# Expert products in four 32-column tiles, a two-part gather, and a ring of 14 weight slots

## The chip, the cores and the metric

The kernel runs on one core of a Trainium2 chip. The metric is the device time of one execution in microseconds. The kernel before took 1646.06 us, the median of three runs (1644.56 to 1650.3). The profiled execution took 1643.47 us, with a span of 1641.8 us from its first to its last instruction. In the rows, PE is the matmul engine, PEld its loading of the stationary operand, DVE, ACT and POOL the vector, scalar and general engines, SP the engine that issues the weight transfers.

## What is computed

Two transformer blocks over 256 tokens of width 1024. Each has a mixer (differential attention, a gated linear recurrence and an mLSTM, gated and merged); the first has a dense feed-forward layer, the second a mixture of eight experts, of which each token uses two. The change lies in the mixture:

```python
def _swiglu(h, w1, w3, w2):
    return (jax.nn.silu(h @ w1) * (h @ w3)) @ w2

def _moe(h, router_w, router_b, w1, w3, w2):
    logits = (h @ router_w).astype(f32) + router_b.astype(f32)
    probs = jax.nn.softmax(logits, axis=-1)
    top_p, top_i = lax.top_k(probs, TOP_K)                  # TOP_K = 2
    top_p = top_p / jnp.sum(top_p, axis=-1, keepdims=True)
    combine = jnp.sum(jax.nn.one_hot(top_i, N_EXPERTS) * top_p[..., None], axis=-2)
    out = jnp.zeros_like(h)
    for e in range(N_EXPERTS):                              # 8
        out = out + combine[..., e:e + 1] * _swiglu(h, w1[e], w3[e], w2[e])
    return out
```

Here `h` is 256 x 1024 (the norm of x, scaled and shifted), and the weights of an expert are 1024 x 2816 twice and 2816 x 1024, all float32.

## The kernel before

**Stages.** Mixer 0, the dense layer and mixer 1 take the first 877 us. Then come the routing (`moe_route`) and the eight experts (`moe_pass`), one after the other, and the output. Up to the end of mixer 1 all large products are made of float32r operands split into a high and a low part; the experts' products are float32 matmuls, which the trace shows as two records each.

**Weights.** An expert reads 35 loads ("raws"), each a transfer of 128 partitions x 2 rows of k x 1024 columns (1 MiB), or x 768 columns (768 KiB) for the last column group of W1 and W3. They come in this order: three column groups g = 0, 1, 2 of 1024, 1024 and 768 columns; in each, four loads of W1, then four of W3; then eleven loads of W2. `Stream.loads` (L78) issues a transfer on SP as soon as a slot of the ring is free. The ring has three pools: `rawa` (4 slots, from the start), `rawb` (5, opened four units before the end of mixer 1, L1696) and `rawc` (7, opened when the pools of the mixer close, L1703). A slot is free again when PE has used its load (`release`). The first nine loads are issued during the end of mixer 1, the next seven when the routing starts.

**Routing.** `moe_route` (L1287) takes the norm's scale `r` per token (a sum on DVE, a power on POOL), makes diagonal matrices `dg` of it on ACT, multiplies x with them into transposed blocks, scales and shifts these (`hf`, by turns on DVE and ACT), and multiplies with the router. The softmax, the two largest and the position of each token within its expert's list follow on DVE, with five small matmuls. Four iotas on POOL (`key`) stand ahead of the power.

**Gather.** `dispatch(e0)` (L1380) builds for two experts at a time a 0/1 matrix of tokens by places, multiplied with `r`; `gather(e0, j)` (L1394) multiplies x (128 tokens x 128 columns, stationary) with it, 256 columns wide, float32, and `xg`, the expert's tokens, scaled and shifted, is written from the sum. The gather for experts 0 and 1 stands ahead of the first expert; that for 2 and 3, 4 and 5, 6 and 7 lies in the W2 loads 4 to 7 of experts 1, 3 and 5.

**Products.** An expert has CAP = 128 places. The tokens are the stationary operand, the weights the moving one. With 64 tokens (HALF) stationary, the array takes two tiles of 64 columns side by side, each with half the load's columns; with 32 (QUART), four tiles of 32, each with a quarter. `passes` (L1458) makes for each load the products of the first 64 tokens always, in two tiles. What is left is decided on the chip by `more` (L1442) from the expert's count, with branches: over 96 tokens, the same again for places 64 to 127 (`half`); 65 to 96, the places 64 to 95 in four tiles (`quart`); at most 64, nothing (`rest`, only the second k-row of the first product). In column group 2 there is no `quart`: 65 to 96 tokens take `half` there, since 768 was not split into quarters (`quarters` is false for g = 2). This is the part of `passes` that makes the tiles:

```python
            def tiles(bank, kind, k, m):
                c = n // (128 // m)
                for q in range(128 // m):
                    PE.matmul(out=bank[m * q:m * q + m, 0:c], lhsT=lhs(kind, k), rhs=w[:, k, c * q:c * q + c],
                              start=first and k == 0, stop=last and k == 1)
```

After each column group the hidden values are transposed for W2 (`transposes`, L1488), three or four blocks of 128 columns for each of the two halves of the places. `scatter` (L1563) multiplies the expert's result back to the tokens' order and adds it to the sum `acc`; it runs in the second load of the next expert.

**Order.** The instructions of the experts are put in order by the scheduler of the tile framework from the code's order; near the end of expert 0 it places a few loads of expert 1 between those of expert 0.

Of the kernel before, what the change touches and what calls it, by code (L numbers as in the profile page):

```python
# [15 lines left out]
OP = mybir.AluOpType  # L16
# [161 lines left out]
MB = dict(small=4, rs=1, rt=1, ix=1, cm=1, fl=1, key=1, dg=1, pg=2, ps=2, xg=1, s=MS, gt=2, gt2=1, dT=2, mfs=2, acc=1)  # L178
RB = 5
RC = 7  # L180
# [10 lines left out]
def _body(ctx, tc, nc, I, out):  # L191
# [1095 lines left out]
    def moe_route():  # L1287
# [67 lines left out]
        cur["moe"] = dict(r=r, rt=rt, cm=cm, key=key, quart=quart)  # L1355

    def moe_pass(stream, off, raw_pool, finish):
# [22 lines left out]
        def dispatch(e0):  # L1380
            m = cur["moe"]
# [12 lines left out]
        def gather(e0, j):  # L1394
            pt = disp[e0]
# [46 lines left out]
        def more(e, half, quart, none=lambda: None):  # L1442
# [4 lines left out]
            with tc.If(num[e] > HALF) as c:  # L1447
                if quart is None:
                    half()
                else:  # L1450
                    with tc.If(num[e] > HALF + QUART) as c2:
                        half()
                    with c2.Else():
                        quart()
# [3 lines left out]
        def passes(e, banks, w, n, lhs, first, last, quarters):  # L1458

            def tiles(bank, kind, k, m):  # L1460
                c = n // (128 // m)
                for q in range(128 // m):
                    PE.matmul(out=bank[m * q:m * q + m, 0:c], lhsT=lhs(kind, k), rhs=w[:, k, c * q:c * q + c],  # L1463
                              start=first and k == 0, stop=last and k == 1)

            def rest():
                tiles(banks[0], 0, 1, HALF)

            def half():
                for k in range(2):  # L1470
                    tiles(banks[1], 1, k, HALF)
                rest()

            def quart():
                for k in range(2):
                    tiles(banks[1], 2, k, QUART)
# [264 lines left out]
```

## Time and profile before

| | |
|---|---|
| median of three runs | 1646.06 us (1644.56 to 1650.3) |
| profiled execution | 1643.47 us, span 1641.8 us |
| PE busy over the span | 1535.2 us (94%) |
| DVE, ACT, POOL busy | 764.9, 575.7 and 42.5 us |
| moved by the transfers | 459.25 MB, mean 280 GB/s |
| first product of expert 0, of expert 7 | 901.87 us, 1521.44 us from the span's start |
| last product of expert 7 | starts at 1626.14 us |

PE is busy nearly throughout, but that share hides that the transfers run at over 400 GB/s in a part of the expert stage and not in others. So the stage is read stretch by stretch: which of PE and DMA has no pause there. Matmul records overlap one another, so that a mean duration of one is more than its part of the time; the time of a run of records divided by their count gives the price.

### The profile page before, as it was taken

What the parts mean: (1) busy time and instruction counts of PE and PEld (TensorE: products, weight loads), DVE (VectorE), ACT (ScalarE), POOL (GpSimd) and SP (SyncE); (2) the same over time, 40 slices, a digit from 0 to 9 for tenths busy, and PEclk for the clock granted to TensorE, in tenths of its full rate; (3) what the DMA queues carried; (4) which work ended last, traced back from release to release, by engine and by line L of the source; (5) the groups of instructions that cost most, each with busy time, mean ns of one, the idle gap of its engine ahead of it and who ended that gap; (6) DMA issues with size and microseconds to landing.
All of it is one profiled execution on the core that took longest, in us unless ns stands there. A gap on an engine that the chain in (4) does not pass through costs nothing. (4 is left out here: it accounts for less than half of the span.)

```text
span 1641.8 us, 25655 instructions
## 1 busy us (share of the span) xinstructions
PE 1535.2 (94%) x10586; PEld 1069.2 (65%) x10586; DVE 764.9 (47%) x1226; ACT 575.7 (35%) x904; POOL 42.5 (3%) x54
## 2 busy tenths in 40 slices
PE   3999999989999899999997999999999988987997
PEld 2999899989998899999996333433334322322332
DVE  7898788755877559865764010211012111111201
ACT  3576557645444487765752010100001000100000
POOL 2001020000000000001000000000000000000000
PEclk9999999999999999999998999999999999999999
DMA  9656777436789633654467799999899999999990
GB/s 361 231 177 217 244 267 259 155 103 226 240 296 320 228 129 129 219 168 154 155 214 299 260 352 354 407 406 321 319 329 407 403 408 405 407 403 407 404 372 36
DMA packets 162776, 459.25 MB, mean 280 GB/s; under 512 B 11454, under 2 KB 19716, under 8 KB 162600
## 3 DMA queue, kind: packets, MB, share of 16 engines
q1 hardware_dynamic: 162408, 456.55, 75.7%
q8 instruction: 140, 2.29, 0.6%
q14 instruction: 36, 0.29, 0.1%
q0 software_dynamic: 192, 0.11, 0.0%
HBM read 455.58 MB, written 1.05 MB: 278 GB/s over the span
## 5 line engine op out<-in xcount | busy, mean ns | idle before, releaser
L1463 PE MATMUL pm<-rawa,xg 128*64 128x512 f32 (+2 forms) x2368 | 417.8, 522 | 21.1 <-DMA rawa<-in_moe_w 18.6
L113 DVE TENSOR_TENSOR wl<-rawa,wh 128x1024 fp32r<-128x1024 f32 (+1 forms) x243 | 293.9, 1215 | 103.1 <-ACT wh L112 102.2
L112 ACT ACTIVATE wh<-rawa 128x1024 fp32r<-128x1024 f32 (+1 forms) x243 | 255.2, 1054 | 229.9 <-PE pm L518 117.3
L1463 PEld LDWEIGHTS pm<-rawa,xg 128*64 128x64 f32 (+1 forms) x2368 | 141.6, 131 | 280.0 <-issue 225.9
L517 PE MATMUL pm<-hh,wh 128*128 128x256 f32 x992 | 285.4, 288 | 4.8 <-ACT hh L499 4.6
L518 PE MATMUL pm<-hl,wh 128*128 128x256 f32 x992 | 283.8, 287 | 0.9 <-DVE hl L500 0.9
L519 PE MATMUL pm<-hh,wl 128*128 128x256 f32 x992 | 283.0, 286 | 1.5 <-DVE wl L113 1.5
L517 PEld LDWEIGHTS pm<-hh,wh 128*128 128x128 f32 x992 | 189.0, 191 | 8.1 <-ACT hh L499 4.8
L519 PEld LDWEIGHTS pm<-hh,wl 128*128 128x128 f32 x992 | 189.1, 191 | 2.4 <-DVE wl L113 1.9
L518 PEld LDWEIGHTS pm<-hl,wh 128*128 128x128 f32 x992 | 189.3, 191 | 1.9 <-DVE hl L500 1.4
L1463 PE MATMUL px<-rawa,gt 128*64 128x512 f32 x704 | 168.0, 600 | 12.5 <-DMA rawa<-in_moe_w 12.3
L1534 DVE TENSOR_TENSOR esg<-esg,pm 128x512 f32<-128x512 f32 (+1 forms) x48 | 29.5, 641 | 297.7 <-PE pm L1463 297.4
L531 PE MATMUL pm<-wl,hh 128*128 128x256 f32 x448 | 128.7, 287 | 1.6 <-DVE wl L113 1.6
L530 PE MATMUL pm<-wh,hh 128*128 128x256 f32 x448 | 128.8, 288 | 0.0
L532 PE MATMUL pm<-wh,hl 128*128 128x256 f32 x448 | 127.8, 285 | 0.0
L1463 PEld LDWEIGHTS px<-rawa,gt 128*64 128x64 f32 x704 | 46.1, 136 | 107.8 <-issue 83.8
L393 DVE SCALAR_TENSOR_TENSOR macc<-rawm,csil,macc 128x1024 f32<-128x1024 f32 x74 | 94.6, 1279 | 30.8 <-DMA rawm<-in_w_mod 30.1
L531 PEld LDWEIGHTS pm<-wl,hh 128*128 128x128 f32 x448 | 85.1, 190 | 2.0 <-DVE wl L113 1.8
L1561 DVE COPY ys<-pm 128x512 f32<-128x512 f32 x8 | 5.5, 691 | 173.2 <-PE pm L1463 93.9
L532 PEld LDWEIGHTS pm<-wh,hl 128*128 128x128 f32 x448 | 85.0, 190 | 0.2 <-issue 0.2
L530 PEld LDWEIGHTS pm<-wh,hh 128*128 128x128 f32 x448 | 85.0, 190 | 0.0
L1497 ACT ACTIVATE gt<-px 128x512 f32<-128x512 f32 (+1 forms) x24 | 13.5, 564 | 197.3 <-PE px L1495 197.3
(370 smaller groups left out, 1940.6 us busy)
## 6 DMA issues: line engine op xcount, KB each, us to landing
rawa<-in_moe_w SPq DMA_DIRECT2D x216, 1024.0 KB, 17.1
rawa<-in_w_in SPq DMA_DIRECT2D x68, 1024.0 KB, 6.3
rawa<-in_moe_w SPq DMA_DIRECT2D x64, 768.0 KB, 12.0
rawm<-in_w_mod SPq DMA_DIRECT2D x80, 512.0 KB, 7.6
rawa<-in_ffn_w SPq DMA_DIRECT2D x29, 1024.0 KB, 7.6
rawa<-in_w_branch SPq DMA_DIRECT2D x12, 1024.0 KB, 5.7
rawa<-in_w_out SPq DMA_DIRECT2D x8, 1024.0 KB, 5.7
rawa<-in_w_mod SPq DMA_DIRECT2D x7, 1024.0 KB, 10.2
```

Source lines behind the costliest of these rows:

```text
L112: nc.scalar.activation(out=hv, in_=src, func=AF.Copy)
L113: nc.vector.tensor_sub(out=lv, in0=src, in1=hv.bitcast(F32))
L393: V.scalar_tensor_tensor(out=st["acc"], in0=src[:, 0], scalar=csil[:, k:k + 1], in1=st["acc"], op0=OP.mult, op1=OP.add)
L517: PE.matmul(out=o, lhsT=wh, rhs=xh[:, k], start=(k == 0), stop=False)
L518: PE.matmul(out=o, lhsT=wh, rhs=xl[:, k], start=False, stop=False)
L519: PE.matmul(out=o, lhsT=wl, rhs=xh[:, k], start=False, stop=(k == nk - 1))
L530: PE.matmul(out=o, lhsT=xh[:, k, c], rhs=wh, start=(k == 0), stop=False)
L531: PE.matmul(out=o, lhsT=xh[:, k, c], rhs=wl, start=False, stop=False)
L532: PE.matmul(out=o, lhsT=xl[:, k, c], rhs=wh, start=False, stop=(k == nk - 1))
L1463: PE.matmul(out=bank[m * q:m * q + m, 0:c], lhsT=lhs(kind, k), rhs=w[:, k, c * q:c * q + c], start=first and k == 0, stop=last and k == 1)
L1497: A.activation(out=gT[g][:, i], in_=pv, func=AF.Copy)
L1534: V.tensor_tensor(out=gt[g][:, b, c], in0=gt[g][:, b, c], in1=hp[1][b][:, c], op=OP.mult)
```

## The change

1. All products of the experts are made in four tiles of 32 columns. For the kinds of 64 tokens (first and second half of the places), tiles 0 and 1 take tokens 0 to 31 and 32 to 63 with the first half of the load's columns, tiles 2 and 3 the same with the second half. Each tile streams as many columns as before (512, or 384 in group 2); there are four matmuls where there were two.
2. `quart` exists in group 2 as well, with 192 columns a tile. The hidden values of that group then lie in another arrangement, so the transposes of the second half (`odd`) have a branch of their own for 65 to 96 tokens: two transposes and two half-high products, one with `ident` and one with `turn`, the identity rotated by 32 columns.
3. The gather takes x times r in a high and a low part, float32r (`xh`, `xl`), with a 0/1 matrix in float32r: per block two products in place of one float32 one. The parts are made once in `moe_route`, on ACT and DVE; the copy of `r` that was kept falls away.
4. The ring has 14 slots in place of 16 (`RC`, 7 to 5).

```diff
-RC = 7
+RC = 5
@@ moe_route
-        r0, dg = norm_scale(Sp)
-        r = M.tile([128, 2], F32, name="rs", tag="rs")
-        V.tensor_copy(out=r, in_=r0)
+        turn = M.tile([128, CAP], F32, name="turn", tag="turn")
+        G.tensor_copy(out=turn[:, 0:CAP - QUART], in_=ident[:, QUART:CAP])
+        G.tensor_copy(out=turn[:, CAP - QUART:CAP], in_=ident[:, 0:QUART])
+        r, dg = norm_scale(Sp)
...
+        xh = M.tile([128, 2, D], F32R, name="xrh", tag="xrh")
+        xl = M.tile([128, 2, D], F32R, name="xrl", tag="xrl")
+        for b in range(2):
+            A.activation(out=xh[:, b], in_=x[:, b], func=AF.Copy, scale=r[:, b:b + 1])
+            V.scalar_tensor_tensor(out=xl[:, b], in0=x[:, b], scalar=r[:, b:b + 1], in1=xh[:, b].bitcast(F32),
+                                   op0=OP.mult, op1=OP.subtract)
@@ dispatch
-                p_ = M().tile([128, 2, CAP], F32, name="pg", tag="pg")
-                idx = index(b, e0, 2)
-                for i in range(2):
-                    V.tensor_scalar(out=p_[:, i], in0=iota, scalar1=idx[:, i:i + 1], scalar2=m["r"][:, b:b + 1],
-                                    op0=OP.is_equal, op1=OP.mult)
+                p_ = M().tile([128, 2, CAP], F32R, name="pg", tag="pg")
+                V.tensor_tensor(out=p_, in0=index(b, e0, 2).unsqueeze(2).to_broadcast([128, 2, CAP]),
+                                in1=iota.unsqueeze(1).to_broadcast([128, 2, CAP]), op=OP.is_equal)
@@ gather
-                    PE.matmul(out=pv[:, k2], lhsT=x[:, b, c], rhs=pt[b].rearrange("p a s -> p (a s)"),
-                              start=(b == 0), stop=(b == 1))
+                    for i, src in enumerate((m["xh"], m["xl"])):
+                        PE.matmul(out=pv[:, k2], lhsT=src[:, b, c], rhs=pt[b].rearrange("p a s -> p (a s)"),
+                                  start=(b == 0 and i == 0), stop=(b == 1 and i == 1))
@@ passes
-            def tiles(bank, kind, k, m):
-                c = n // (128 // m)
-                for q in range(128 // m):
-                    PE.matmul(out=bank[m * q:m * q + m, 0:c], lhsT=lhs(kind, k), rhs=w[:, k, c * q:c * q + c],
-                              start=first and k == 0, stop=last and k == 1)
+            def tiles(bank, kind, k):
+                parts = 4 if kind == 2 else 2
+                c = n // parts
+                for q in range(4):
+                    t = q if kind < 2 else 0
+                    h = q * parts // 4
+                    o = QUART * (t % 2)
+                    PE.matmul(out=bank[QUART * q:QUART * q + QUART, 0:c], lhsT=lhs(kind, k)[:, o:o + QUART],
+                              rhs=w[:, k, c * h:c * h + c], start=first and k == 0, stop=last and k == 1)
...
-            more(e, half, quart if quarters else None, rest)
+            more(e, half, quart, rest)
@@ transposes
+                    def odd():
+
+                        for c in range(2):
+                            PE.transpose(out=pv[:, c], in_=src[:, c * 64:c * 64 + 128], identity=ident)
+                        PE.matmul(out=pv[0:64, 2], lhsT=src[:, 128:192], rhs=ident, start=True, stop=True)
+                        PE.matmul(out=pv[64:128, 2], lhsT=src[:, 0:64], rhs=cur["moe"]["turn"], start=True, stop=True)
+
+                    if i == 1 and g == 2:
+                        more(e, blocks, odd, blocks)
+                    else:
+                        blocks()
```

On PE, a load of expert 0 with 1024 columns stands like this before. The matmuls after the two compares are, in turn, the branch for over 96 tokens, the one for 65 to 96 (eight narrow ones and two wide), and the one for at most 64:

```order
L1463 MATMUL pm<-rawa_9331,xg 64x512 x2
L1447 COMPARE_AND_BRANCH
L1451 COMPARE_AND_BRANCH
L1463 MATMUL pm<-rawa_9331,xg 64x512 x6
L1451 UNCONDITIONAL_BRANCH
L1463 MATMUL pm<-rawa_9331,xg 32x256 x8
L1463 MATMUL pm<-rawa_9331,xg 64x512 x2
L1451 UNCONDITIONAL_BRANCH
L1463 MATMUL pm<-rawa_9331,xg 64x512 x2
L1447 UNCONDITIONAL_BRANCH
```

The same load on PE now:

```order
L1470 MATMUL pm<-rawa_9331,xg 32x512 x4
L1453 COMPARE_AND_BRANCH
L1454 COMPARE_AND_BRANCH
L1470 MATMUL pm<-rawa_9331,xg 32x512 x12
L1454 UNCONDITIONAL_BRANCH
L1470 MATMUL pm<-rawa_9331,xg 32x256 x8
L1470 MATMUL pm<-rawa_9331,xg 32x512 x4
L1454 UNCONDITIONAL_BRANCH
L1470 MATMUL pm<-rawa_9331,xg 32x512 x4
L1453 UNCONDITIONAL_BRANCH
```

All shapes have 32 columns now; 20 matmuls in the program became 32, of which a light expert runs 8 in place of 4, and one with 65 to 96 tokens 16 in place of 12.

A load of column group 2 on PE (768 columns), before:

```order
L1463 MATMUL pm<-rawa_10629,xg 64x384 x2
L1447 COMPARE_AND_BRANCH
L1463 MATMUL pm<-rawa_10629,xg 64x384 x6
L1447 UNCONDITIONAL_BRANCH
L1463 MATMUL pm<-rawa_10629,xg 64x384 x2
L1447 UNCONDITIONAL_BRANCH
```

And a load of that group now:

```order
L1470 MATMUL pm<-rawa_11273,xg 32x384 x4
L1453 COMPARE_AND_BRANCH
L1454 COMPARE_AND_BRANCH
L1470 MATMUL pm<-rawa_11273,xg 32x384 x12
L1454 UNCONDITIONAL_BRANCH
L1470 MATMUL pm<-rawa_11273,xg 32x192 x8
L1470 MATMUL pm<-rawa_11273,xg 32x384 x4
L1454 UNCONDITIONAL_BRANCH
L1470 MATMUL pm<-rawa_11273,xg 32x384 x4
L1453 UNCONDITIONAL_BRANCH
```

The second compare and the branch with 192 columns are new; the program has 32 matmuls for the load where it had 10.

On DVE in the routing, from the norm's blocks (`hf`) to the first operation on the router's sums (`rt`), before:

```order
L1301 COPY rs<-rr 128x2
L486 TENSOR_SCALAR hf<-px,acol_114,modc_112 128x256 x4
L1317 TENSOR_TENSOR rt<-pm,rb_82 128x8 x2
L1318 MAX rt<-rt 128x8 x2
L1319 TENSOR_TENSOR rt<-rt 128x2x8
```

And now:

```order
L486 TENSOR_SCALAR hf<-px,acol_114,modc_112 128x256
L1360 SCALAR_TENSOR_TENSOR xrl<-x_76,rr,xrh 128x1024
L486 TENSOR_SCALAR hf<-px,acol_114,modc_112 128x256 x3
L1360 SCALAR_TENSOR_TENSOR xrl<-x_76,rr,xrh 128x1024
L1318 TENSOR_TENSOR rt<-pm,rb_82 128x8 x2
```

The two operations that make the low part stand between the first and the second `hf` and behind the fourth. On ACT the two that make the high part stand between `dg` and the first `hf`; on POOL the two copies for `turn` stand between the iotas and the power.

## Rows read from the trace of the kernel before

**Rows 1.** Windows: stretch, length, busy time by engine (records), PEclk, DMA share, GB/s
```profile
877.00:902.00 25.00, 19.63 (x108) 17.86 (x109) 11.40 (x53) 5.45 (x9) 0.00 (x0) 0.74 0.70 283
902.00:1012.00 110.00, 108.66 (x824) 37.88 (x827) 9.24 (x21) 7.67 (x13) 0.00 (x0) 1.00 0.87 309
1012.00:1080.00 68.00, 67.60 (x352) 29.07 (x346) 14.21 (x30) 8.24 (x16) 0.00 (x0) 1.00 1.03 406
1080.00:1202.00 122.00, 121.60 (x600) 45.37 (x598) 11.97 (x23) 6.46 (x13) 0.00 (x0) 1.00 0.93 340
1329.00:1521.00 192.00, 160.42 (x722) 53.41 (x720) 24.35 (x49) 14.56 (x29) 0.00 (x0) 0.99 1.03 406
1521.00:1627.00 106.00, 105.13 (x812) 36.48 (x812) 14.28 (x19) 6.30 (x12) 0.00 (x0) 1.00 0.75 294
```
**Rows 2.** Timeline of PE, end of expert 4: start, duration, records [idle before, releaser]
```profile
1329.72 1.94 PE L1463 MATMUL px<-rawa,gt 128*64 128x512 f32 x8 [0.51 <-DMA rawa<-in_moe_w]
1332.27 1.94 PE L1463 MATMUL px<-rawa,gt 128*64 128x512 f32 x8 [0.61 <-DMA rawa<-in_moe_w]
```
**Rows 3.** Chain that ended last, in expert 7: start, duration, records
```profile
1577.89 15.63 PE pm L1463 x96
...
1605.06 1.00 PE pm L1463 x16
1606.06 1.87 PE px L1463 x8
...
1627.85 3.33 PE px L1570 x20
```
**Rows 4.** Timeline of PE: W2 of expert 1, then a run in expert 2
```profile
1068.12 12.24 PE L1463 MATMUL px<-rawa,gt 128*64 128x512 f32 x56
...
1090.48 24.25 PE L1463 MATMUL pm<-rawa,xg 128*64 128x512 f32 x112
```
**Rows 5.** Groups by shape: gather at 893 to 902, at 1054 to 1069: busy, mean
```profile
L1401 PE MATMUL px<-pg,x 128*128 128x256 f32 x32 | 8.9, 448 | 2.5 <-DVE pg L1387 2.5
L1401 PE MATMUL px<-pg,x 128*128 128x256 f32 x32 | 7.9, 389 | 0.0
```
**Rows 6.** Timeline of PE in mixer 1: float32r products
```profile
789.92 0.29 PE L517 MATMUL pm<-hh,wh 128*128 128x256 f32 x1
790.04 0.28 PE L518 MATMUL pm<-hl,wh 128*128 128x256 f32 x1
```
**Rows 7.** Timeline of the routing, 874 to 886: start, duration, engine, operation
```profile
874.67 0.45 POOL L1294 IOTA key<- 128x128 f32 x2 [50.81 <-DMA rawa<-in_moe_w]
...
875.47 0.71 POOL L273 TENSOR_TENSOR rr<-rv,mhalf 128x2 f32<-128x2 f32 x1
...
876.22 0.69 ACT L461 ACTIVATE dg<-ident,rr 128x128 f32<-128x128 f32 x2 [1.67 <-POOL rr L273]
...
879.21 0.54 DVE L486 TENSOR_SCALAR hf<-px,acol,modc 128x256 f32<-128x256 f32 x1 [2.82 <-PE px L473]
879.79 0.56 ACT L488 ACTIVATE hf<-px,modc,acol 128x256 f32<-128x256 f32 x1 [2.88 <-DVE hf L486]
880.12 0.54 DVE L486 TENSOR_SCALAR hf<-px,acol,modc 128x256 f32<-128x256 f32 x1 [0.37 <-PE px L473]
...
882.77 0.54 DVE L486 TENSOR_SCALAR hf<-px,acol,modc 128x256 f32<-128x256 f32 x1 [1.22 <-PE pm L1308]
...
885.15 0.39 DVE L1317 TENSOR_TENSOR rt<-pm,rb 128x8 f32<-128x8 f32 x2 [1.84 <-PE pm L1308]
```
**Rows 8.** Groups of the page, whole span: operations on 128x1024 (busy, mean ns)
```profile
L112 ACT ACTIVATE wh<-rawa 128x1024 fp32r<-128x1024 f32 (+1 forms) x243 | 255.2, 1054 | 229.9 <-PE pm L518 117.3
...
L393 DVE SCALAR_TENSOR_TENSOR macc<-rawm,csil,macc 128x1024 f32<-128x1024 f32 x74 | 94.6, 1279 | 30.8 <-DMA rawm<-in_w_mod 30.1
```
**Rows 9.** Instruction queue at 1213 to 1521, at 893 to 1637: packets, MB, share
```profile
q8 instruction: 41, 0.67, 0.9%
...
q8 instruction: 88, 1.44, 0.8%
```

More of the change, by code (lines that the diff above doesn't have):

```diff
@@ L175, in tile @@
         return self.pool.tile(shape, dt, name=name, tag="dg" if name == "dg" else "s" if tag == "t" else tag)
-MB = dict(small=4, rs=1, rt=1, ix=1, cm=1, fl=1, key=1, dg=1, pg=2, ps=2, xg=1, s=MS, gt=2, gt2=1, dT=2, mfs=2, acc=1)
+MB = dict(small=4, xrh=1, xrl=1, turn=1, rt=1, ix=1, cm=1, fl=1, key=1, dg=1, pg=2, ps=2, xg=1, s=MS, gt=2, gt2=1, dT=2, mfs=2, acc=1)
 RB = 5
-RC = 7
+RC = 5
 def build(tc, ins, out):
@@ L1394, in gather @@
         def gather(e0, j):
+            m = cur["moe"]
             pt = disp[e0]
@@ L1447, in more, with passes @@
             with tc.If(num[e] > HALF) as c:
-                if quart is None:
+                with tc.If(num[e] > HALF + QUART) as c2:
                     half()
[L1450 to L1454, printed above, removed]
+                with c2.Else():
+                    quart()
             with c.Else():
                 none()
-        def passes(e, banks, w, n, lhs, first, last, quarters):
-            def tiles(bank, kind, k, m):
-                c = n // (128 // m)
-                for q in range(128 // m):
-                    PE.matmul(out=bank[m * q:m * q + m, 0:c], lhsT=lhs(kind, k), rhs=w[:, k, c * q:c * q + c],
-                              start=first and k == 0, stop=last and k == 1)
+        def passes(e, banks, w, n, lhs, first, last):
+            def tiles(bank, kind, k):
[7 more added lines that the diff above has]
+                              rhs=w[:, k, c * h:c * h + c], start=first and k == 0, stop=last and k == 1)
             def rest():
-                tiles(banks[0], 0, 1, HALF)
+                tiles(banks[0], 0, 1)
             def half():
                 for k in range(2):
-                    tiles(banks[1], 1, k, HALF)
+                    tiles(banks[1], 1, k)
                 rest()
@@ L1475, in quart @@
                 for k in range(2):
-                    tiles(banks[1], 2, k, QUART)
+                    tiles(banks[1], 2, k)
                 rest()
-            tiles(banks[0], 0, 0, HALF)
-            more(e, half, quart if quarters else None, rest)
+            tiles(banks[0], 0, 0)
+            more(e, half, quart, rest)
         def expert(e):
@@ L1493, in transposes, with blocks @@
                     pv = p.rearrange("p (c s) -> p c s", c=4)[:, 0:nb]
-                    for c in range(nb):
-                        PE.transpose(out=pv[:, c], in_=gt[g][:, i, c * 128:c * 128 + 128], identity=ident)
+                    src = gt[g][:, i]
+                    def blocks():
+                        for c in range(nb):
+                            PE.transpose(out=pv[:, c], in_=src[:, c * 128:c * 128 + 128], identity=ident)
+                    def odd():
[7 more added lines that the diff above has]
+                        blocks()
                     if i == 0:
@@ L1542, in fn @@
                         y.extend((ps_x(), hp[1][1]))
-                    passes(e, y, hi[0], 1024, lambda kind, k: hidden(2 * ch + k, kind), ch == 0, ch == 10, True)
+                    passes(e, y, hi[0], 1024, lambda kind, k: hidden(2 * ch + k, kind), ch == 0, ch == 10)
                     if ch == 1:
```

14 lines of the change are left out of this document (7 added, 7 removed).

## The prediction

> **What bounds the kernel now.** I read the expert stage first by its stretches [rows 1], then the engine that waits in the middle of it, then the chain that ended last. The last expert starts at 1521 and the chain runs from there to the end on PE; between 1012 and 1521 the transfers move 405 GB/s nearly throughout, but not before it and not between 1080 and 1202 [rows 1]. Which products run shows the routing: expert 0 and expert 7 have between 65 and 96 tokens (sets of 16 narrow records, as in [rows 3]), expert 2 more than 96 (twice the records of [rows 2] for a load), the other five at most 64. So there are three regimes.
>
> Up to the end of expert 2, at 1202, PE sets the pace. PE is busy 108.7 of 110 us and 121.6 of 122 us there while DMA moves 309 and 340 GB/s [rows 1]: the ring of weight slots is full, and a transfer waits for a slot. From about 1329 to 1521 DMA sets it: a load of 1 MiB arrives every 2.55 us, and PE works 1.94 us on it and waits 0.6 us [rows 2]. In expert 7 it is PE again: busy 105.1 of 106 us, DMA at 294 GB/s [rows 1], and the chain there is nothing but its products [rows 3]. Time saved in the first regime is kept, since the transfers that follow start as much earlier; saved in experts 3 to 6 it is lost in the wait for the next load; saved in expert 7 it is kept, as long as DMA can follow.
>
> **The change, part by part.** *The price of a product now.* A float32 matmul is two records. With two tiles of 64 columns, four records of 512 columns take 24.25/28 = 0.866 us [rows 4], so a pair that runs side by side takes 0.433. A load of a light expert costs 4 pairs, 1.73 us; one of expert 2 costs 8, 3.46. In experts 0 and 7 the chain shows a period of 1.00 + 1.87 = 2.87 us for a load [rows 3]: 16 narrow records (4 sets of four) and 8 wide ones (4 pairs). The wide ones should take 1.73 and took 1.87; the narrow sets stream half the columns, so 4 x 0.217 = 0.87, and took 1.00. The two surpluses, 0.14 and 0.13, stand on both sides of each change from 64 to 32 columns and back. Expert 2 has its branch at the same place, keeps one shape and has no surplus [rows 4], so I charge them to the change of shape.
>
> *All products in 32 columns.* Every load now has the same shape throughout, and the moving columns per set stay 512, with four tiles side by side in place of two. Four side by side are in the trace already, the 16 narrow records. I take 0.433 for a set of four at 512 columns, so light and heavy loads keep their time, and a load of experts 0 and 7 takes 4 x 0.433 + 4 x 0.217 = 2.60: 0.27 saved on each of 16 + 11 loads, 7.3 us an expert.
>
> That a set of four costs no more than a pair is the step on which the most hangs. The Trainium skill (TensorE: Matmul & The Clock Gate, section Measured speedup vs the span model) speaks against it: three column tiles of 512 columns gave 2.38 times one, not 3. As an estimate from that page a set would take 0.433 x 3/2.38 = 0.55 us, a light load 2.2 us, and the sum would end near 1710. This case's narrow sets took 0.25 us at most, surplus included, where that ratio on 0.217 would give 0.27; the trace doesn't bear it out.
>
> *Quarters in the narrow group.* Of the 8 loads of 768 KiB per expert, experts 0 and 7 now do two full halves: 16 records of 384 columns, 15.63/96 x 16 = 2.60 us [rows 3]. The second half becomes four tiles of 192 columns, half the time: 1.30 + 0.65 = 1.95. Saved: 0.65 x 8 = 5.2 us an expert. If a short set had a floor at the 0.217 of the 256-column ones, it would be 3.5. The changed transposes (two and two products in place of three) cost under 0.5 us an expert and I leave them out.
>
> *The gather.* 16 float32 products (32 records) become 32 single-record float32r ones. In expert 1 the 32 records take 7.9 us [rows 5]; float32r products of 128x256 start 0.12 us apart in the projections [rows 6], so 32 take 3.84: 4.0 saved in expert 1, which PE bounds. In experts 3 and 5 the same gain vanishes in the wait for DMA. The first gather, ahead of expert 0, takes 8.9 us [rows 5] since the clock is partly at its lower level, 0.74 of full on average in that stretch [rows 1]; 3.84/0.74 = 5.2, so 3.7 saved (between 1.2, all at half clock, and 5.1).
>
> *What this puts on the path to the first product.* On POOL, two copies that make `turn` stand ahead of the power that gives the norm's scale; nearest rows, two iotas in 0.45 us and a small tensor-tensor of 0.71 [rows 7]: 0.3 to 1.4, taken 0.5. On ACT, two activations of 1.05 us [rows 8] go between `dg` and the first `hf`, where ACT idles 2.88 us [rows 7]: hidden, with 0.8 to spare. On DVE two of 1.28 us [rows 8]: the second fits in the 1.84 us of idle ahead of `rt`; the first stands between the first and the second `hf`, where 0.37 is idle, and delays by 0.9 the second, but the fourth waits 1.22 for PE anyway [rows 7]: 0 to 0.9, taken 0.5. Sum +1.0 (0.3 to 2.3).
>
> *The ring, 16 to 14.* When expert 2 ends, the ring is full in both kernels, and DMA has two loads less in hand. From there DMA needs 2 x 1.048576 MB/0.406 = 5.2 us more until expert 7 can start. Before that the smaller ring must carry expert 1: PE takes its 35 loads in some 64 us, DMA brings about 26 in that time, so the lead of 14 falls to about 4 or 5 and expert 2 fills it up again; it holds, not by much.
>
> *The code.* The order has 20 matmuls in each load's branches (10 in the narrow group), afterwards 32: some 690 an expert become about 1,190, 1.7 times the code. Queue 8, which fetches it, moved 41 blocks of 16 KB in the DMA-bound stretch, 0.9% of 16 engines over 308 us, 1.08 us a block [rows 9]. 29 more are 31 us of one engine's time: 2 us if all 16 share it, 4 if the blocks fall on half of them, since a load is complete only with its slowest part. Taken: 4 (0 to 8).
>
> **The sum.** Until expert 2 ends: +1.0 - 3.7 - 7.3 - 5.2 - 4.0 = -19.2. Ring +5.2, code +4: expert 7 starts 10.0 earlier. Expert 7: -7.3 - 5.2 = -12.5; it then needs 93 us of PE, and its transfers 27 x 2.58 + 8 x 1.94 = 85, so PE still ends it, just. The tail after the last product (scatter, finish, output) is untouched. Together -22.5: from the profiled execution, 1643.47 (span 1641.8), to 1621; that run is 2.6 below the median, so the median goes to **1624**.
>
> **Rivals.** *Four tiles cost more than two* (the other side). If the surplus of 0.13 on the four narrow sets belongs to sets of four, 0.035 each, and not to the change of shape, all sets pay it. Experts 0 and 7 then gain nothing in the wide groups and about 3 us in the narrow one; expert 1 loses 35 x 4 x 0.035 = 4.9 and expert 2 9.8. Up to expert 2: +1.0 - 3.7 - 3 + 4.9 - 4.0 + 9.8 = +5; ring and code +9; expert 7 -3: about +12, **1658**. It turns slower from about 0.03 us a set. Against it: the 64-column pairs of the same period pay 0.14 too. Chance 0.10. A set as slow as the page's ratio would fall under this case.
>
> *The code fetch cannot follow.* A light expert that PE bounds would use a block every 3.3 us (about 19 blocks in 64 us); now it uses 10 or 11 in 68, and all 88 blocks of the stage came in 744 us [rows 9], so no row shows such a pace. At 5 us a block, expert 1 takes 32 us longer and experts 3 to 6 9 each: +77 - 22 = +55, **1701**; at 4.4 the gain is just gone. For it speaks also the Trainium skill (Runtime: NRT & Kernel Launch, section Instruction fetch mechanics): a taken branch out of the prefetched window stalls for a fetch. The light experts jump over a load's unused branches now without a gap, 56 records of seven loads in 12.24 us [rows 4], and the jump grows by about half. Chance 0.08, half of it about no change.
>
> *The ring runs dry before expert 2 fills it.* If the lead in expert 1 is 4 loads less than I count (expert 0 frees its slots out of order), PE waits 4 x 2.58 = 10 us: **1634**, chance 0.08.
>
> *No cost of code, and a cheaper start:* -28, **1618** or a little less, is within the forecast's own range. That the change does nothing is excluded: the shapes and products are other instructions.
>
> **How the numbers follow.** Forecast 0.74 (with 1612 to 1632 as its own range), dry ring 0.08, four tiles dearer 0.10, fetch 0.08. The range that holds 8 in 10 takes the forecast and the dry ring: 1610 to 1640. Faster by over 0.3% (5 us, about what a measurement of this kernel tells from no change): 0.74 + 0.08 = 0.82; within: 0.04; slower: 0.10 + 0.04 = 0.14.
>
> **What would show it.** Right: no surplus around the 256-column sets and a period of 2.60 in experts 0 and 7; four records of 512 columns side by side every 0.433 us; a narrow load of 1.95; gathers of about 4 and 5 us; expert 2 ending near 1183 and expert 7 starting near 1511, both from the span's start. Wrong: PE gaps in experts 1 and 2 at branches (fetch), a wait for DMA before 1180 (ring), or a longer interval of transfers than 2.6 us between expert 4 and 6 (code, dearer than I took it). If expert 7 shows waits for DMA, its saving is cut and the end is set by the last transfer.

## The result and the profile after

The changed kernel takes 1744.64 us (median of 4 runs, 1741.4 to 1749.58) where the kernel before, run beside it, takes 1645.31 (1640.93 to 1650.3): the ratio is 1.0607, with a 95% interval of 1.0579 to 1.0635. It is 6% slower. The forecast was 1624, in a range of 1610 to 1640.

The stretches say where. The windows of the kernel before, as in [rows 1] but cut at the same places for both kernels: experts 0 and 1, expert 2, experts 3 to 6, and expert 7 to the end (stretch, length, busy time of PE, PEld, DVE, ACT, POOL with records, PEclk, DMA share, GB/s):

```profile
901.90:1080.20 178.30, 176.55 (x1171) 67.07 (x1172) 23.55 (x51) 15.91 (x29) 0.00 (x0) 1.00 0.93 346
1080.20:1201.70 121.50, 121.10 (x598) 45.21 (x596) 11.88 (x23) 6.42 (x12) 0.00 (x0) 1.00 0.93 339
1201.70:1521.40 319.70, 286.49 (x1338) 102.78 (x1334) 49.38 (x101) 29.40 (x57) 0.00 (x0) 0.99 1.02 399
1521.40:1641.00 119.60, 108.99 (x836) 38.72 (x836) 19.01 (x27) 6.50 (x13) 0.00 (x0) 0.97 0.69 269
```

The same four of the changed kernel:

```profile
901.80:1100.70 198.90, 173.79 (x1796) 71.11 (x1799) 22.76 (x48) 16.39 (x30) 0.00 (x0) 0.97 0.90 335
1100.70:1223.70 123.00, 121.44 (x1164) 41.38 (x1160) 11.92 (x23) 6.42 (x12) 0.00 (x0) 1.00 0.85 298
1223.70:1627.20 403.50, 308.59 (x2464) 99.84 (x2460) 48.60 (x98) 28.86 (x56) 0.00 (x0) 0.95 0.94 343
1627.20:1744.00 116.80, 100.27 (x1187) 45.85 (x1179) 19.57 (x27) 7.02 (x13) 0.00 (x0) 0.95 0.58 207
```

The first product of expert 0 starts where it did. Experts 0 and 1 take 20.6 us more, expert 2 1.5 more, experts 3 to 6 83.8 more, and expert 7 with the tail 2.8 less: together 103 us. The largest part lies where the prediction had let the transfers, not PE, set the pace: in experts 3 to 6 the transfers ran at 399 GB/s before, and now they run at 343.

What PE waits for in experts 3 to 6, before (the answer on waits: total us, times, longest):

```profile
PE pm L1463 <- DMA rawa<-in_moe_w: 18.0, 29, 2.1
PE px L1463 <- DMA rawa<-in_moe_w: 12.3, 16, 2.2
```

And after:

```profile
PE pm L1470 <- issue: 64.8, 34, 3.3
PE px L1470 <- issue: 26.4, 16, 3.1
PE px L1505 <- issue: 2.3, 1, 2.3
```

The wait for weights is gone, the ring is full; in its place stand 93.5 us of "issue", time in which PE waits for nothing that the profile shows. In the timeline the pauses are regular (changed kernel, expert 3; compare [rows 2, 4]):

```profile
1258.96 3.64 PE L1470 MATMUL pm<-rawa,xg 128*32 128x512 f32 x32 [1.89 <-issue]
1265.44 4.47 PE L1470 MATMUL pm<-rawa,xg 128*32 128x512 f32 x32 [2.84 <-issue]
1271.15 0.85 PE L1470 MATMUL pm<-rawa,xg 128*32 128x384 f32 x8 [1.23 <-issue]
```

32 records are two loads of a light expert, so PE passes two branches, makes two loads without a gap, and stops. Two loads are 64 products in the program, of which 16 run. The instruction queue gives the match; its row for experts 3 to 6, of the kernel before and of the changed kernel (packets, MB, share):

```profile
q8 instruction: 43, 0.70, 0.9%
```
```profile
q8 instruction: 74, 1.21, 1.2%
```

74 blocks of 16 KB for four experts are 18.5 for one. A light expert has 35 x 32 = 1120 products in the program and some 63 others: 1183/64 = 18.5. So a pause falls at the end of a block of code. Single packets can be placed by narrow windows: of the stretch shown, one lies at 1262.8 to 1264.0, the next at 1268.6 to 1269.7, the next at 1274.5 to 1275.6, none between. PE goes on at 1265.44 and 1271.15, each time about 1.45 us after a packet has landed. Over the 48 pauses of more than 0.5 us in these experts that distance is 1.2 to 1.6 us, and the next packet starts 3.1 us (median) after PE has gone on. With 1.0 us for the packet that is a cycle of 5.5 us, in which PE has work for 3.5. It looks as if each block is asked for only some time after PE has entered the one before; no run shows the request itself.

The pauses also lower the granted clock. Windows of two runs of 32 records, the first behind a pause of 1.89 us, the second behind one of 2.84:

```profile
1258.90:1262.70 3.80, 3.64 (x32) 0.94 (x32) 0.00 (x0) 0.00 (x0) 0.00 (x0) 1.00 1.05 376
1265.40:1269.90 4.50, 4.46 (x32) 1.18 (x32) 1.29 (x2) 0.00 (x0) 0.00 (x0) 0.66 0.91 311
```

The first ran at the full level (2.4 GHz), the second in part at the lower one (1.2 GHz), and PE's busy time over experts 3 to 6 rose with it (308.6 us from 286.5).

### The profile page after: what moved, and what is told of

Same layout as the page of the kernel before. It is cut to its first block, busy times and chain, and to the rows that moved or that the text cites. A ratio compares the mean times of both kernels' runs of the same rounds, so it can differ in the third digit from the quotient of the medians.

```text
span 1744.4 us, 31009 instructions
## 1 busy us (share of the span) xinstructions
PE 1543.4 (88%) x13240; PEld 1072.8 (62%) x13240; DVE 765.6 (44%) x1219; ACT 577.9 (33%) x906; POOL 44.0 (3%) x56
## 5 line engine op out<-in xcount | busy, mean ns | idle before, releaser
L1470 PE MATMUL pm<-rawa,xg 128*32 128x512 f32 (+3 forms) x4224 | 429.0, 544 | 85.9 <-issue 85.1
L1470 PEld LDWEIGHTS pm<-rawa,xg 128*32 128x32 f32 x4224 | 147.9, 113 | 348.6 <-issue 331.6
L112 ACT ACTIVATE wh<-rawa 128x1024 fp32r<-128x1024 f32 (+1 forms) x243 | 255.2, 1054 | 230.7 <-PE pm L518 117.5
L1470 PE MATMUL px<-rawa,gt 128*32 128x512 f32 x1408 | 179.2, 610 | 34.9 <-issue 34.8
L1470 PEld LDWEIGHTS px<-rawa,gt 128*32 128x32 f32 x1408 | 45.6, 112 | 136.0 <-issue 130.0
```

The costliest lines, as they stand in the source:

```text
L112: nc.scalar.activation(out=hv, in_=src, func=AF.Copy)
L1470: PE.matmul(out=bank[QUART * q:QUART * q + QUART, 0:c], lhsT=lhs(kind, k)[:, o:o + QUART], rhs=w[:, k, c * h:c * h + c], start=first and k ...
```

## The experiments

The theory: **the fetch of PE's code** sets the pace of the light experts; what counts is how many products stand in the program, run or not. The rivals: PE is slower because **twice as many products run**; each **branch** costs; or **ring, gather or quarters** carry part of the loss. A table first; the columns for experts 3 to 6 are the length of that stretch, the blocks of code in it and PE's pauses put down to issue. A total for which no interval is given below is the time of one execution.

| kernel | products per wide load, in the program / run in a light expert | experts 3 to 6, us | blocks | issue, us | total, us |
|---|---|---|---|---|---|
| before | 20 / 4 | 319.7 | 43 | 0.3 | 1643 to 1646 |
| changed | 32 / 8 | 403.5 | 74 | 93.5 | 1744.6 |
| dead_code | 32 / 4 | 405.6 | 76 | 93.7 | 1810.6 |
| light_bare | 8 / 8 (experts 1, 3 to 6) | 320.1 | 20 | 0 | 1636.6 |
| half_bytes | 32 / 8 | 321.4 | 75 | 31.5 | 1625.4 |
| quarter_bytes | 32 / 8 | 289.6 | 74 | 8.7 | 1582.9 |
| rest_only | 20 / 4 | 322.3 | 48 | 3.6 | 1643.0 |
| shared_24 | 24 / 8 | 356.9 | 58 | 4.5 | 1681.1 |
| nest_18 | 18 / 4 | 322.5 | 44 | 0.6 | 1638.0 |

**Code that never runs.** To the kernel before (not the changed one), a branch is added that is never taken:

```diff
             with tc.If(num[e] > HALF) as c:
+                if dead is not None:
+                    with tc.If(num[e] > CAP):
+                        dead()
...
+            def dead():
+                for _ in range(6 if quarters else 11):
+                    for q in range(2):
+                        PE.matmul(out=banks[1][HALF * q:HALF * q + HALF, 0:n // 2], lhsT=lhs(1, 0),
+                                  rhs=w[:, 0, n // 2 * q:n // 2 * q + n // 2], start=False, stop=False)
```

> The kernel before, with products added to each load that never run: in the branch for over 64 tokens stands a further branch for over 128, with 12 products (22 in the narrow group), so that PE's program has as many products per load as the changed kernel, 32, and what runs is what ran before (experts 0, 2 and 7 run one more compare per load). Theory (the fetch of PE's code sets the pace: a block of 16 KB, 64 float32 products with their weight loads, every 5.5 to 5.7 us): experts 1 and 3 to 6 take about 101 us each as in the changed kernel, in place of 80 and 72 to 87; total 1735 to 1765 us, with pauses of 1.2 to 3 us on PE put down to issue. Rival (the number of products that run, or the four tiles themselves, sets the pace): the time stays at 1645, at most 10 more for the compares.

1810.6 us. Its window of experts 3 to 6:

```profile
1263.90:1669.50 405.60, 309.81 (x1340) 108.87 (x1338) 49.02 (x100) 29.06 (x56) 0.00 (x0) 0.95 0.93 342
```

What PE waits for there, and the row of the instruction queue:

```profile
PE pm L1466 <- issue: 72.9, 41, 3.3
PE px L1466 <- issue: 19.1, 10, 4.0
```
```profile
q8 instruction: 76, 1.25, 1.2%
```

The same 1340 records as before (1338), in two tiles, and yet the length, the pauses, the blocks and the clock of the changed kernel. Neither the number of products that run nor the four tiles can be the cause. The total is 46 us above the range that I gave, since experts 0, 2 and 7 pass the added code as well (expert 2 took 139.5 us in place of 121.5).

**The light experts without the other paths.**

```diff
+            if e in (1, 3, 4, 5, 6):
+                none()
+                return
             with tc.If(num[e] > HALF) as c:
```

> The changed kernel, but experts 1 and 3 to 6 have in the program only the path for at most 64 tokens, without compares and without the two other paths; what runs there is what ran. Theory (code fetch): 280 products per light expert in place of 1120, some 5.5 blocks in place of 18.5, so that expert 1 is bound by PE again (about 66 us in place of 100) and experts 3 to 6 by the transfers (about 72 us in place of 101), no pause put down to issue; total 1610 to 1630 us. Rival (running twice as many products costs PE the time): 1744 as the changed kernel. A cost of the branches themselves would make this fast too; the kernel with code that never runs tells that apart.

1636.6 us. The window of experts 3 to 6, and what PE waits for there:

```profile
1193.20:1513.30 320.10, 281.98 (x2462) 88.59 (x2454) 50.83 (x99) 29.46 (x57) 0.00 (x0) 1.00 1.02 402
```
```profile
PE pm L1473 <- DMA rawa<-in_moe_w: 16.0, 26, 2.1
PE px L1473 <- DMA rawa<-in_moe_w: 14.5, 18, 2.2
```

All 2462 records of the changed kernel run, at full clock, and PE waits for weights again as before. So running twice as many products is free, and sets of four are as cheap as pairs. The total is 7 us above the range: experts 0 and 7 still carry all paths and their pauses (expert 7 took 110.8 us up to PE's last record, 110.1 before).

**How much the weights' traffic matters.** The changed kernel with half of the bytes (half of the columns, read twice), and with a quarter (one k-row of these). Both leave out weights, so that they compute something else; PE's program and the products that run are those of the changed kernel:

```diff
-                        raw = piece(stream, W, g * 1024, n, 2 * i, 2, raw_pool)
+                        raw = piece(stream, W, g * 1024, n // 2, 2 * i, 2, raw_pool)
...
-                    h = q * parts // 4
+                    h = (q * parts // 4) % (parts // 2)
```

> The changed kernel with half of the weights' bytes: each load of an expert brings the first half of its columns, and the products read those twice. PE's program and the products that run are the same. Theory A (a block's 5.7 us is the way of one request and one answer, whatever the weight transfers do): light experts stay at 98 to 103 us, total 1730 to 1745. Theory B (the code's blocks queue behind the weight transfers): the pace of blocks improves with the traffic, 4.5 us a block or less, light experts at 83 us or less, total 1660 or less.

> The changed kernel with a quarter of the weights' bytes: each load of an expert brings one of its two k-rows and of that the first half of its columns, and the products read those four times. PE's program and the products that run are the same. In half_bytes a block of code started 1.2 us (median) after PE had entered the one before it, in the changed kernel 3.1 us. Theory B (the blocks wait behind the weight transfers on the queues): the wait falls to 0.6 us, with 1.0 us of transfer and 1.45 us until PE goes on a block takes 3.1 us, which is less than PE works on two loads, 3.46: light experts come to 66 to 72 us with few pauses, total 1550 to 1585. Theory C (half_bytes gained from its other order of loads, or from a PE that no longer shares something else): the light experts stay at 77 to 87 us, total 1610 to 1630.

1625.4 and 1582.9 us. The window of experts 3 to 6 with half of the bytes and PE's longest wait there, then the same two views with a quarter:

```profile
1204.70:1526.10 321.40, 286.89 (x2526) 105.38 (x2519) 49.49 (x99) 29.58 (x58) 0.00 (x0) 0.99 0.69 218
```
```profile
PE pm L1470 <- issue: 19.8, 22, 2.0
```
```profile
1195.00:1484.60 289.60, 277.52 (x2528) 110.13 (x2520) 49.56 (x99) 29.49 (x58) 0.00 (x0) 1.00 0.43 124
```
```profile
PE pm L1470 <- issue: 5.2, 10, 1.1
```

The same code and the same products, and the cycle of a block falls from 403.5/74 = 5.5 us to 321.4/75 = 4.3 and 289.6/74 = 3.9, where PE hardly pauses. What shortens is the way to the packet. From PE's restart to the start of the next packet it is 3.1 us, then 1.6 with half of the bytes and 1.4 with a quarter (medians of the 48, 24 and 8 pauses of more than 0.5 us in experts 3 to 6; taken from expert 1 on, half_bytes gives the 1.2 of the expectation above). The packet's own 1.0 us and the 1.45 us behind it don't change. So the code comes the later, the more weights move: theory B. But the way did not fall to 0.6 us, as was expected for the quarter; there PE works nearly without a pause (8.7 us in 289.6), so that 3.9 us a block is mostly PE's own pace. The order of some loads differs between the three kernels, and what that does is not separated.

**Everything but the four tiles.** The 64-place products in two tiles again (the tiles of the kernel before, in the changed kernel):

```diff
             def tiles(bank, kind, k):
+                if kind < 2:
+                    for q in range(2):
+                        PE.matmul(out=bank[HALF * q:HALF * q + HALF, 0:n // 2], lhsT=lhs(kind, k),
+                                  rhs=w[:, k, n // 2 * q:n // 2 * q + n // 2], start=first and k == 0, stop=last and k == 1)
+                    return
                 parts = 4 if kind == 2 else 2
                 c = n // parts
```

> The changed kernel with its products of 64 tokens in two tiles of 64 columns again; the gather in two parts, the quarters in the narrow group with the changed transposes and the ring of 14 stay. 20 products per load in the program, 11.9 blocks for a light expert, 66 us, which is just expert 1's pace on PE. Theory (the code of the four tiles alone made the loss): by the prediction's own terms +1.0 - 3.5 - 3.0 (expert 0's narrow group with the surplus at the change of shape) - 4.0 + 5.2 + 1 - 3.0 = -6.3, so 1639 (1633 to 1647). Rival (ring, gather or quarters carry part of the loss): 1660 or more.

1642.99 us, ratio 0.9998 (0.9986 to 1.001). The four tiles made the whole loss, by their code, as dead_code and light_bare show; the other three parts together are worth nothing measurable. With 20 products in the narrow loads too (before: 10) the code still shows, in experts 0 and 1 (before: 1.3 us of issue):

```profile
PE pm L1466 <- issue: 3.2, 3, 1.8
PE px L1466 <- issue: 1.5, 1, 1.5
```

**Fewer products in the program, the same ones run.** First the shared second k-row ahead of the branch (the edit shown), or behind it:

```diff
-            def rest():
-                tiles(banks[0], 0, 1)
...
-            tiles(banks[0], 0, 0)
-            more(e, half, quart, rest)
+            for k in range(2):
+                tiles(banks[0], 0, k)
+            more(e, half, quart)
```

> The changed kernel with the second k-row of the first 64 places made ahead of the branch, once, in place of in each of its three paths: 24 products per load in the program in place of 32; the same products run, and the same compares. Theory (code fetch, 0.085 us per product in the program and some 63 other products per expert): a light expert needs (840 + 63)/64 = 14.1 blocks, 77 us; experts 1 and 3 to 6 lose 24 us each, expert 7 its 5 us of pauses; total 1744 - 120 - 5 = 1619, 1610 to 1635. Rivals (each branch costs a fixed time; the products that run cost it): 1744.

> The changed kernel with the second k-row of the first 64 places made once, behind the branch, in place of at the end of each of its three paths: 24 products per load in the program in place of 32, in the order in which the changed kernel runs them, and the last reader of a load's slot is a product again (in shared_24 it was the branch, and PE ran dry after each load). Theory (code fetch at 5.5 us a block under full weight traffic): 14.1 blocks for a light expert, 78 us for experts 1, 3 and 4, then the transfers set about 86 us; expert 7 without pauses at about 98 us; total 1630 to 1645. Rival (each branch, or the four tiles, cost the time): 1735 to 1750.

1681.1 and 1685.1 us, 46 and 40 above their ranges: some 60 of the 99 us of loss are gone, not all. The pauses of issue are nearly gone (4.5 us in experts 3 to 6 of shared_24 in place of 93.5), as the theory wants; in their place is a new wait, the same in both kernels (shared_24, expert 3):

```profile
1220.68 1.92 PE L1470 MATMUL pm<-rawa,xg 128*32 128x512 f32 x16 [0.17 <-PEq L1453]
1222.77 1.92 PE L1470 MATMUL pm<-rawa,xg 128*32 128x512 f32 x16 [0.17 <-PEq L1453]
```

In both kernels a load takes 2.09 us where the products alone take 1.73. PE's sequencer passes a semaphore instruction at the branch (L1453), after the last product has ended, and only then starts the next load; the traces of both kernels have 180 such instructions at that line, that of the changed kernel 5. The path for at most 64 tokens has become empty in these kernels. I took the place of the branch for the reason and moved the row behind it; the wait stayed, so that was wrong. The same with the second 64 places in two tiles (kind 1, 20 products), with the new gather and ring, and with the old ones:

> As tail_24, with the second 64 places (expert 2) in two tiles of 64 columns: 20 products per load in the program, 11.9 blocks for a light expert, 66 us. Theory (code fetch): no pause on PE; experts 0 and 7 gain 12.5 each as predicted for the four tiles, expert 1 its 4.0, the start 2.5, expert 2 loses 9.4 (35 changes of shape at 0.27), the ring costs 5.2, code 1: -16, so 1629 (1620 to 1640). If the fetch costs more than that, experts 1 and 3 show pauses put down to issue and the total is over 1645.

> As tail_20, with the gather of the kernel before (float32, no high and low part) and its ring of 16 slots. Against tail_20 it gives back the gather's 7.5 us (3.5 at the start, 4.0 in expert 1) and saves the ring's 5.2: theory 1631 (1622 to 1642), 2 us above tail_20. If the ring of 14 costs nothing, it is 7 above; if the gather brings nothing, 5 below.

Both missed, by 39 and 47 us: 1667.6 us (ratio 1.0146, 1.0126 to 1.0166) and 1678.0 (1.0205, 1.0187 to 1.0223). The empty path is there again, and expert 2 pays the changes of shape, 133.2 us for 121.5. The kernel with the old gather and ring is 10.3 us behind the other, where 2 were forecast; why it is so much here stays open. But look at expert 7 with the tail in tail_20, to be set against the 119.60 us of the kernel before:

```profile
1557.90:1666.00 108.10, 96.29 (x1182) 41.55 (x1181) 18.88 (x26) 6.42 (x12) 0.00 (x0) 0.97 0.69 270
```

Up to PE's last record that is 98.8 us for 110.1: of the 12.5 us forecast for four tiles with quarters, 11.3 are there as soon as the code is small enough.

Then kernels in which no path is empty, since one product of the shared row stands in each path, and every second load has its branch first:

```diff
+            def piece():
+                if flip:
+                    tiles(banks[0], 0, 0, slice(0, 1))
+                else:
+                    tiles(banks[0], 0, 1, slice(-1, None))
...
+            if not flip:
+                tiles(banks[0], 0, 0)
+                tiles(banks[0], 0, 1, slice(0, -1))
+            more(e, path(1), path(2), piece)
+            if flip:
+                tiles(banks[0], 0, 0, slice(1, None))
+                tiles(banks[0], 0, 1)
```

> The changed kernel with 18 products per load in the program: the first 64 places in two tiles of 64 columns and made once, all but one product, which stands in each of the three paths (so that no path is empty: in the kernels with shared rows an empty path cost a semaphore instruction, for which PE ran dry, 0.36 us a load). Every second load has the branch first and the shared products behind it, so that two quarters' sets stand next to each other and the shape changes half as often. Theory (code fetch; 10.8 blocks, 59 us for a light expert): no pauses put down to issue; experts 0 and 7 gain 4.1 each in the narrow group and 3.7 from the changes of shape, expert 1 4.0, the start 2.5, the ring costs 5.2, fewer blocks save 1: -14 to -19, 1627 (1620 to 1636). Rival (the drain is the branch's own, not the empty path's): light experts on PE at 2.09 us a load, total 1650 or more.

> As split_18, with the first 64 places in four tiles of 32 columns (the second half of expert 2 in two): 22 products per load, 13.0 blocks, 71.6 us for a light expert. Theory (code fetch): expert 1 takes 5 us longer than on PE alone, expert 0 and 7 gain the full 12.5 each, expert 2 loses 4.7 at half the changes of shape: 1630 (1622 to 1642), with a few pauses of issue in expert 1 and 3. Rival (drain of the branch): 1660 or more.

> As split_18, with the gather and the ring of 16 of the kernel before. Theory: gives back the gather's 6.5 to 7.5 and saves the ring's 5.2: 1629 (1621 to 1639), within 5 us of split_18.

1644.7 us (ratio 1.0005, 0.9988 to 1.0021), 1649.4 (1.0038, 1.0022 to 1.0054) and 1649.2 (1.003, 1.0013 to 1.0046). The wait at the branch is gone (0.2 us in experts 3 to 6 of split_18), so it belonged to the empty path. The rarer changes of shape do bring what was forecast: in W2 of expert 7 two loads of split_18 take 5.44 us (5.47 forecast, 2 x 2.87 before), as its chain shows:

```profile
1622.56 1.86 PE pm L1471 x32
1624.42 3.58 PE px L1471 x16
```

Expert 7 with the tail is 6.2 us shorter there than before (113.4 for 119.6), but experts 0 and 1 take 179.1 us for 178.3, and experts 3 to 6 324.3 for 319.7. Two things in the trace account for a part in experts 0 and 1: in some loads of W1 and W3 a product that is cut off from its pair runs alone (the last wide record ahead of the narrow ones stands 0.43 us behind the one before it), and the scatter is busy 7.3 us in place of 3.9. The rest is not explained. In split_22 13 blocks an expert are too many once more: 20.0 us of issue in experts 3 to 6.

Last, the second k-row once for both paths over 64 and once for the third, two tiles, no pair split (`inner` holds the second branch):

```diff
+            def second(kind):
+                for k in range(2):
+                    tiles(banks[1], kind, k)
...
+                with tc.If(num[e] > HALF + QUART) as c2:
+                    second(1)
+                with c2.Else():
+                    second(2)
+
+            tiles(banks[0], 0, 0)
...
+                with tc.If(num[e] > HALF) as c1:
+                    tiles(banks[0], 0, 1)
+                    inner()
+                with c1.Else():
+                    tiles(banks[0], 0, 1)
```

> As rest_only (64 places in two tiles), with the second k-row of the first 64 places made once for both paths over 64 tokens, and once for the path at most 64: 18 products per load in the program in place of 20, no path empty, no tile pair split. Theory (code fetch): 10.8 blocks for a light expert, 59 us, so that the 4.6 us of pauses that rest_only has in experts 0 and 1, and those in expert 3, go: 1637 (1631 to 1643). Rival (those pauses cost nothing in the end, the transfers set the time): 1643 as rest_only.

> As nest_18, with the gather and the ring of 16 of the kernel before, so that against the kernel before only the quarters in the narrow group (3.0 us each in experts 0 and 7) and the smaller program are left: 1637 (1632 to 1643). If the gather and the ring of 14 together gain, as split_18 against split_18_r16 says (4.5 us), it is 1641 where nest_18 is 1637.

1637.95 us, ratio 0.9963 (0.9947 to 0.998), and 1639.89, ratio 0.9986 (0.9975 to 0.9998). nest_18 is 0.4% faster than the kernel before, and its interval lies below 1. Its windows, cut as above, and those of nest_18_r16 for experts 0 and 1 and for 3 to 6:

```profile
898.20:1072.10 173.90, 171.56 (x1236) 63.47 (x1237) 22.97 (x48) 16.32 (x30) 0.00 (x0) 1.00 0.91 345
1072.10:1193.40 121.30, 120.90 (x600) 45.35 (x598) 11.94 (x23) 6.42 (x12) 0.00 (x0) 1.00 0.96 355
1193.40:1515.90 322.50, 282.08 (x1340) 98.00 (x1336) 48.80 (x99) 29.45 (x57) 0.00 (x0) 0.99 1.02 402
1515.90:1633.00 117.10, 105.97 (x903) 37.00 (x903) 18.97 (x27) 6.46 (x13) 0.00 (x0) 0.98 0.71 277
```
```profile
901.30:1079.00 177.70, 175.80 (x1240) 66.73 (x1241) 24.32 (x52) 16.55 (x30) 0.00 (x0) 1.00 0.93 346
1199.50:1518.40 318.90, 284.41 (x1338) 102.32 (x1334) 49.38 (x101) 29.40 (x57) 0.00 (x0) 1.00 1.02 400
```

Against the kernel before, experts 0 and 1 gain 4.4, expert 7 2.5, experts 3 to 6 lose 2.8. Another 3.7 us of the profiled execution lie ahead of expert 0, whose start differs between kernels for reasons that no run separates, so not all of the gain is the change's. Against rest_only, experts 0 and 1 take 4.0 us less (173.9 for 177.9), with 2.0 us of issue for 4.7: a part of what rest_only lacked was the code. The medians of the two nest kernels are 2 us apart and their intervals overlap: the new gather and the smaller ring about cancel.

## Why the prediction was wrong

- **The code (taken +4, 0 to 8): the step that failed.** It counted the blocks rightly (1.7 times the code) and priced them wrongly, as a load on the transfer engines, 1.08 us of one engine each. PE needs the block itself: the next one is 5.5 us away under full traffic, and a light expert uses one up in 3.5. The term measured 20.6 + 83.8 us and the lost gains of experts 0, 1 and 7 on top. The row that I read as reassuring [rows 9], 41 blocks in 308 us, gives a mean of need over a stretch in which PE waited for weights. In a busy stretch of the kernel before, 1225 to 1250 us, the window and the row of the instruction queue are:

```profile
1225.00:1250.00 25.00, 24.58 (x135) 9.70 (x131) 3.57 (x8) 2.91 (x6) 0.00 (x0) 1.00 1.03 408
```
```profile
q8 instruction: 5, 0.08, 1.3%
```

  The five blocks stand 5.7 to 6.2 us apart, with PE busy 24.6 of 25 us: the kernel already ran near the pace that the fetch keeps in the changed kernel, and a program 1.7 times as large could not fit.
- **That time "saved in experts 3 to 6" is "lost in the wait for the next load"** holds for time saved. It doesn't hold for time added: 30 us of waiting were all the slack there, and the code needed 84 more. Expert 3, from 1202 to 1276, which the three regimes leave out, had no slack at all: PE was busy 73.5 of 74.2 us.
- **The rival had it.** "The code fetch cannot follow" named the place, the mechanism and the sign, with 19 blocks an expert; at 5 us a block it gave 1701, at the measured 5.5 a light expert takes the 101 us seen. (Its sum, +77, counts 9 us for five experts where it names four; with four it is +68 and 1692.) Its chance, 0.08, was too small: it says itself that no row of the kernel before shows the pace that the change needs, a block every 3.3 us, and that should have weighed more.
- The Trainium skill (Runtime: NRT & Kernel Launch, section Instruction fetch mechanics), named there, has blocks fetched ahead in sequence, mostly hidden, and a stall where a branch leaves the fetched window. The trace agrees with a stall, but not with its place, and "mostly hidden" fits the kernel before (0.3 us of issue in experts 3 to 6) and not the changed one (93.5): there PE pauses 51 times on issue for 140 loads and 74 blocks, at the blocks' ends and not at each branch, and dead_code pauses alike.
- **Four tiles cost no more than two: right.** light_bare runs 2462 records in the time of 1338, and in the changed kernel's expert 7 four wide and four narrow sets take 1.72 + 0.86 = 2.58 us (forecast 2.60), the surplus at the change of shape gone. The chain there, against [rows 3]:

```profile
1689.49 2.05 issue
...
1725.02 0.86 PE pm L1470 x16
1725.88 1.72 PE px L1470 x16
```

  The Trainium skill's ratio for three column tiles (TensorE: Matmul & The Clock Gate, section Measured speedup vs the span model) gave the estimate of 0.55 us a set. That doesn't hold here: a set takes 1.72/4 = 0.43. The ratio itself, against one tile alone, no run here measures.
- **Experts 0 and 7 (-12.5 each): right in size, not reached.** 11.3 in expert 7 of tail_20; expert 0 was not measured by itself. In the changed kernel PE would use a block there every 5.2 us (96.6 busy us for 18.5 blocks), and 5.2 us of pauses of issue stand in expert 7 alone; of the 12.5 us, 2.8 are left with the tail.
- **Gather and ring (-4.0, -3.7, +5.2): right within some us.** Between the two nest kernels, experts 0 and 1 gain 3.8 us by the gather and experts 3 to 6 lose 3.6 by the ring; the medians differ by 2 (by 4.5 and 10.3 in the split_18 and tail_20 pairs). The trace of nest_18 shows no wait of PE for a load in experts 0 to 2, so the ring of 14 does not run dry. The float32r products stand 0.12 us apart in the changed kernel too, as read from [rows 6], and its two gathers are busy 5.7 and 4.6 us in place of 8.9 and 7.9. What the start of expert 0 gains can't be told: its place moves by 7 us between kernels that are alike up to there (898.0 in shared_24, 904.8 in tail_20).
- **Routing (+1.0):** too small to be seen beside that.

## What to carry to other kernels

Count the instructions of a stretch, those that a branch skips included, and set the blocks that they need against the time in which the engine works them off; compare that with the shortest spacing of code blocks that the trace shows under the same traffic, since a mean need says nothing of the limit. In this kernel, where the transfers saturate, a smaller program was worth more than fewer products run. When shared work is taken out of branches, look whether a path is left empty, and leave something in it.

## What the runs showed of the hardware

- Where PE waits for its code, a block of 16 KB comes every 5.5 us under 343 GB/s of weights and 4.3 at 218; at 124 it is 3.9, with PE nearly without pause. Skipped code is fetched like code that runs: 76 blocks in dead_code, 43 in the kernel before, for the same products. PE goes on about 1.45 us after the packet has landed, at all three.
- PE's granted clock fell with these pauses: 0.95 over experts 3 to 6 (1.00 in light_bare), 1.00 in a run behind a pause of 1.89 us, 0.66 in one behind 2.84 us.
- A path of a branch without a product costs 0.36 us a load (2.09 for 1.73): a semaphore instruction at the branch, which PE passes only after its last product has ended.
- A change between tiles of 64 and of 32 columns costs 0.13 to 0.14 us: half as many changes make two loads of expert 7 5.44 us in place of 5.74, none make one 2.58 in place of 2.87.
